# Attention probabilities left unscaled, their reciprocal sums folded into the transposes

## The chip, the cores and the metric

The kernel runs on one core of one Trainium2 chip. The metric is the device time of one execution in microseconds (us). Engines are named as the profile names them: PE is TensorE (PEld its weight loads), DVE is VectorE, ACT is ScalarE, POOL is GpSimd, SP is the engine that issues the DMAs.

## The reference, cut to what matters

One inference step of a two-layer backbone on 128 context tokens and 512 latent tokens, in float32. In each layer a mixer of three head groups (mLSTM, gated linear attention, latent attention) is followed by an output projection, a layer norm, a SwiGLU feed-forward part and a second layer norm. The change is inside the third head group:

```python
def block(args):
    qnb, qrb = args
    s = jnp.einsum('bhqd,bhkd->bhqk', qnb, k_nope) + jnp.einsum('bhqr,bkr->bhqk', qrb, k_rope)
    p = jax.nn.softmax(s.astype(jnp.float32) * A_SCALE, axis=-1)
    return jnp.einsum('bhqk,bhkv->bhqv', p.astype(v.dtype), v)
```

There are 8 heads. The 512 latent queries (four tiles of 128) read 640 keys: 128 cached ones and the 512 latent ones. The 128 context queries read the 128 context keys only.

## The kernel before, in words

A layer goes through the input projections, the mLSTM group, the gated linear group, the latent attention (four pairs of heads), the output projection (`accd` tiles), and the feed-forward part (`pg`, `pu`, `accd`). `mm` (L60) is every product, `act` (L46) every ScalarE operation, `tt` (L49) every elementwise operation of two tensors, `ts` (L53) one with a scalar for each partition. Three products of `F32R` pairs for each step (`mm3`) make up most of PE's work; the value products `O`, the scan products `hnum` and `go` and the broadcasts `Mb` are products of plain `F32` tiles.

For a head h and a query tile t of 1 to 4, `scores` does this: six `F32R` products make the scores in the PSUM tile `sp` (128 x 640, two buffers); DVE takes the negated row maximum `nm`; ACT writes the exponentials into `Pt` (128 x 640) and the row sums into `sums`; DVE makes the reciprocal `rc`; and `Pt` is multiplied by `rc` in place, on POOL for t of 1 to 3 and on DVE for t of 4. `ptile` then makes, for each of five key tiles kt, the transposed probabilities `PT` (128 keys x 512 queries): four PE transposes, one for each query tile, into a PSUM tile with two buffers, then one copy to SBUF, on ACT for even kt and on DVE for odd kt. `values` multiplies `PT` with the values `Vt` into `O`. `prompt_scores` does the same for the context queries with the tiles `Pp` and `PTp`; it scales `Pp` on POOL, and the change leaves it alone.

The loop at the end of `mixer` goes over four pairs of heads; what order the instructions get on each engine is set by the framework's scheduler, which moves them between pairs. Before the attention, a few tiles are prepared: `cko` (a copy of the context latents that goes out by DMA) and `nc_` (the cached latents and rotary keys, which come in by DMA). They lie in the pool `qa`, on the side of SBUF that also gets the attention's tiles. `g0` is the pool of the gated linear group, whose tag `kx` (two buffers, `gla_ends`) is used before.

Of the kernel before, what the change touches and what calls it, by code (L numbers as in the profile page):

```python
# [6 lines left out]
F32 = mybir.dt.float32  # L7
# [28 lines left out]
def build(nc, tc, I, O, dbg=None, layers=L, stop=None):  # L36
    V, S, P, T = nc.vector, nc.scalar, nc.gpsimd, nc.tensor

    def dma(out, in_):
        return nc.sync.dma_start(out=out, in_=in_)  # L40

    def pool(name, bufs=1, **kw):
        return tc.tile_pool(name=name, bufs=bufs, reuse_waits="tile", **kw)

    def act(out, in_, f, **kw):
        return S.activation(out=out, in_=in_, func=f, **kw)  # L46

    def tt(out, a, b, op, e=V):
        return e.tensor_tensor(out=out, in0=a, in1=b, op=op)  # L49

    def ts(out, a, s1, s2, o0, o1=None, e=V):
        if o1 is None:
            return e.tensor_scalar(out, a, s1, None, op0=o0)  # L53
        return e.tensor_scalar(out, a, s1, s2, op0=o0, op1=o1)
# [4 lines left out]
    def mm(out, lhsT, rhs, start=True, stop=True):  # L59
        return T.matmul(out, lhsT, rhs, start=start, stop=stop)  # L60

    def mm3(out, a, b, start, stop):
        mm(out, a[0], b[0], start, False)
        mm(out, a[0], b[1], False, False)
        mm(out, a[1], b[0], False, stop)
# [8 lines left out]
    ADD, SUB, MUL, MAX, MIN = ALU.add, ALU.subtract, ALU.mult, ALU.max, ALU.min  # L74
# [28 lines left out]
    def pa(name="pa"):  # L103
        return pt("a", name)

    def pb(name="pb"):
        return pt("b", name)

    def pq(name="pq"):
        return pt("q", name)  # L110
# [18 lines left out]
    ident = cst.tile([128, 128], F32, name="ident")  # L129
# [185 lines left out]
    def hsplit(h, l, src, e=V):  # L315
        act(h, src, AF.Copy)
        tt(l, src, h.bitcast(F32), SUB, e=e)
# [5 lines left out]
    def mixer(l, hT, adas, pm0, ws=None):  # L323
# [11 lines left out]
        g0 = g0s.enter_context(pool(f"glas{l}"))  # L335
# [57 lines left out]
        else:  # L393
            todo = [(g, f) for g in range(2) for f in first]
            for part in (todo[:5], todo[5:]):
                accs = [pt("aabbb"[i], "acc") for i in range(len(part))]
                for kk in range(4):
                    for acc, (g, ((src, M), (wh, wl), dst)) in zip(accs, part):
                        h, lo = hT[g]
# [74 lines left out]
        for i, (src, sc) in enumerate(((I_, -1.0), (e_, KSC), (eg, 1.0))):  # L474
            tr = pb("tokT")
# [21 lines left out]
        for t in range(NT):  # L497
            tr = pb("kT")
# [3 lines left out]
        def pos2tile(d, j):  # L502
            return 0 if j == 0 else (j if d == 0 else 5 - j)
# [5 lines left out]
        for j in range(0, 4):  # L509
            for d in range(2):  # L510
                t = pos2tile(d, j)
# [21 lines left out]
        for t in range(NT):  # L533
# [17 lines left out]
            for p in range(2):  # L551
                sq = pq("qk")
                for hh in range(2):
                    h = 2 * p + hh
# [164 lines left out]
        for j in range(0, 4):  # L719
            next(q2)  # L720
            for d in range(2):
                t = pos2tile(d, j)
# [133 lines left out]
        qp = lat2.enter_context(pool(f"qa{l}", side="right"))  # L856
# [4 lines left out]
        tr = pa("ckT")  # L861
        T.transpose(tr[:, 0:128], akv[:, 0:128], ident)
        T.transpose(tr[:, 128:160], misc[0:32, 0:128], ident[0:32, 0:32])
        cko = qp.tile([128, 160], F32, name="cko")
        V.tensor_copy(cko, tr[:, 0:160])
        dma(O["ckv"][l], cko[:, 0:128])
        dma(O["kr"][l], cko[:, 128:160])
        for i in range(2):
            hsplit(cq[0][:, i], cq[1][:, i], acq[i])
        nc_ = qp.tile([128, 128], F32, name="nc_")  # L870
        dma(nc_, I["ckvT"][l])
        for dst, src in ((slice(0, 128), akv[:, 0:128]), (slice(128, 256), nc_), (slice(256, 768), akv[:, 128:640])):
            hsplit(ckv[0][:, dst], ckv[1][:, dst], src)
# [22 lines left out]
        qp = lat2.enter_context(pool(f"qb{l}", side="right"))  # L896
# [58 lines left out]
        Qs, Ps, Pp = {}, {}, {}  # L955
# [37 lines left out]

        def scores(h):
            q, k = Qs[h], Kt[h % 3]
            for t in range(1, NT):
                sp = pq("sp")
                for cc in range(2):
                    tc_, kc = slice(t * 128, (t + 1) * 128), slice(128 + cc * 320, 448 + cc * 320)
                    mm3(sp[:, cc, 0:320], (q[0][:, tc_], q[1][:, tc_]), (k[0][:, kc], k[1][:, kc]), True, True)  # L1000
                nm = qp.tile([128, 1], F32, tag="nm", bufs=4, name="nm")
                V.tensor_reduce(nm, sp[:, :, 0:320], AX.XY, MAX, negate=True)
                Pt = (ap if h % 2 else qp).tile([128, 640], F32, tag="Pt", bufs=5, name="Pt")
                act(Pt.rearrange("p (a b) -> p a b", a=2), sp[:, :, 0:320], AF.Exp, bias=nm,
                    accum_out=sums[:, t, h:h + 1])
                rc = qp.tile([128, 1], F32, tag="rc", bufs=4, name="rc")
                V.reciprocal(rc, sums[:, t, h:h + 1])
                tt(Pt, Pt, rc.to_broadcast([128, 640]), MUL, e=P) if t % 4 else ts(Pt, Pt, rc, None, MUL)
                Ps[h, t] = Pt

        def prompt_scores(p):
            sp = pb("spp")
# [16 lines left out]
        def ptile(h, kt):  # L1029
            tr = pb("PT")  # L1030
            for t in range(1, NT):
                T.transpose(tr[:, (t - 1) * 128:t * 128], Ps[h, t][:, kt * 128:(kt + 1) * 128], ident)  # L1032
            PT = ap.tile([128, 512], F32, tag="PT", bufs=8, name="PT")
            if kt % 2:
                V.tensor_copy(PT, tr)
            else:
                act(PT, tr, AF.Copy)
            return PT

        def values(p, PA):  # L1040
# [24 lines left out]
            for kt in range(NT):  # L1065
                PB[kt] = ptile(2 * p + 1, kt)
                if kt == 0:
                    prompt_T()
                if kt not in (1, 4):
                    continue  # L1070

                ins = None
                ks = (1, 0) if kt == 1 else (4, 3, 2)
                for k in ks:
                    for hh in (1, 0):
                        h = 2 * p + hh
                        with tc.issue_after(ins.ins) if ins else nullcontext():
                            i_ = mm(O_[64 * hh:64 * hh + 64, :], Vt[:, 1 + k, h * 64:(h + 1) * 64], (PA[k], PB[k])[hh],
                                    k == 1, k == 2)
                        ins = ins or i_  # L1080
                if kt == 1:
                    with tc.issue_after(ins.ins):
                        prompt_O()
# [4 lines left out]
        proj(0, True)  # L1088
        run(chain(vals(), rope(1)))
        scores(0)  # L1090
        run(mix_T())
        persist.close()
        am = ExitStack()
        ap = am.enter_context(pool(f"am{l}"))
        for p in range(4):
            scores(2 * p + 1)
            prompt_scores(p)
            PA = [ptile(2 * p, kt) for kt in range(NT)]
            if p < 3:
                proj(p + 1)  # L1100
            values(p, PA)
            if p < 3:
                scores(2 * p + 2)
# [241 lines left out]
    for t in range(NT):  # L1345
        r = p0.tile([128, 1024], F32, tag="xrow", bufs=NT, name="xrow")
        dma(r, xin(t))
        for hf in range(2):
            tr = pb("hTt")
# [14 lines left out]
    for qt in range(NQ):  # L1364
# [19 lines left out]
        tr = ada_[:, 1, qt * KQ * 64:(qt + 1) * KQ * 64]  # L1384
# [19 lines left out]
    for l in range(layers):  # L1404
        mixT = mixer(l, hT, adas if l == 0 else iter(()), pm if l == 0 else None, ws if l == 0 else None)
        hT = tail_half(l, mixT, xin if l == 0 else (lambda t: xsp[t]), adan)
# [143 lines left out]
```

## Time and profile before

| | us |
|---|---|
| median of 3 runs | 1842.28 (1838.88 to 1842.68) |
| the profiled execution, its own time | 1843.47 |
| its span, first to last instruction | 1841.7 |
| PE busy | 1739.3 (94%) |
| DVE busy | 1039.5 (56%) |
| ACT busy | 701.9 (38%) |
| POOL busy | 331.3 (18%) |

The busy time of an engine is the union of its instructions' times. On PE the instructions overlap: the end of a matmul is modelled, and the next one starts before it. So the time between the starts of two matmuls, not the duration of one, tells how long PE was taken by it. A row of the timeline that merges n equal instructions gives the first start and the time to the last end; that time less one duration, over n - 1, is the distance between starts.

### The profile page before, as it was taken

Reading aid. Unit: us, or ns where it says so; the run is one execution under the profiler, and the core shown is the slowest. Engines: PE = TensorE matmul, PEld = TensorE weight load, DVE = VectorE, ACT = ScalarE, POOL = GpSimd, SP = SyncE. Lnnn points to the kernel's source line nnn. Section 1 sums busy time; section 2 is a strip of 40 time slices with the busy share of each in tenths; the row PEclk is TensorE's granted clock in tenths of the full one; section 3 lists DMA queues with packets and bytes.
Section 4 is the critical chain, followed back from the end, with each engine's and each line's share of the span. In section 5 each row is a group of like instructions: output and inputs, shape, how many; then the busy total and the mean of one; then the engine's idle time right before and its main releaser. Section 6 shows DMA issues by size and latency. Waiting matters only on the chain.

```text
span 1841.7 us, 28757 instructions
## 1 busy us (share of the span) xinstructions
PE 1739.3 (94%) x11360; PEld 1528.5 (83%) x11360; DVE 1039.5 (56%) x1888; ACT 701.9 (38%) x1490; POOL 331.3 (18%) x280
## 2 busy tenths in 40 slices
PE   8999988989999999999988999898999999999996
PEld 4877877768999899899878888676789989989995
DVE  3536377757588757564476366776465334333237
ACT  4345465743422122122243556576152212222221
POOL 0002352421430000000032126235026000000003
PEclk9989999999999999999998899999999999999998
DMA  9644431033256445343223223201412222213211
GB/s 323 214 132 144 147 89 41 17 122 109 97 157 204 141 138 162 119 127 97 79 80 123 26 62 96 68 17 38 172 69 92 71 79 81 69 59 95 76 58 57
DMA packets 83830, 190.96 MB, mean 104 GB/s; under 512 B 13864, under 2 KB 29512, under 8 KB 81648
## 3 DMA queue, kind: packets, MB, share of 16 engines
q1 hardware_dynamic: 83696, 189.14, 33.3%
q8 instruction: 89, 1.46, 0.3%
q14 instruction: 45, 0.37, 0.1%
HBM read 174.27 MB, written 5.70 MB: 98 GB/s over the span
## 4 chain that ended last, share of the span: by engine, by line
PE 79%; DVE 9%; DMA 5%; ACT 4%; issue 2%; POOL 2%; SPq 0%; DVEq 0%; ACTq 0%; POOLq 0%
PE accd L60 21%; PE pu L60 16%; PE pg L60 16%; PE acc L60 6%; PE accB L60 5%; PE sp L60 2%; PE O L60 2%; DMA araw<-w_ada 2%; PE ada L60 2%; POOL x L49 1%; PE PT L1032 1%; PE hnum L60 1%; PE ep L60 1%; ACT Pt L46 1%; PE go L60 1%
## 5 line engine op out<-in xcount | busy, mean ns | idle before, releaser
L46 ACT ACTIVATE wh<-raw 128x1024 fp32r<-128x1024 f32 (+2 forms) x193 | 197.3, 1027 | 545.2 <-PE accd L60 229.8
L49 DVE TENSOR_TENSOR wl<-raw,wh 128x1024 fp32r<-128x1024 f32 (+2 forms) x175 | 218.3, 1250 | 305.3 <-ACT wh L46 301.8
L60 PE MATMUL pg<-l,wh 128*128 128x256 f32 (+1 forms) x704 | 219.9, 312 | 8.6 <-DVE l L49 8.6
L60 PE MATMUL pu<-h,wl 128*128 128x256 f32 (+1 forms) x704 | 218.0, 310 | 1.4 <-POOL wl L49 1.4
L60 PE MATMUL pg<-h,wh 128*128 128x256 f32 (+1 forms) x704 | 219.2, 312 | 0.0
L60 PE MATMUL pg<-h,wl 128*128 128x384 f32 (+1 forms) x704 | 219.0, 312 | 0.0
L60 PE MATMUL pu<-l,wh 128*128 128x256 f32 (+1 forms) x704 | 218.3, 310 | 0.0
L60 PE MATMUL pu<-h,wh 128*128 128x256 f32 (+1 forms) x704 | 218.3, 310 | 0.0
L49 POOL TENSOR_TENSOR x<-x,lrow 128x512 f32<-128x512 f32 (+1 forms) x22 | 42.0, 1932 | 826.2 <-PE hTt L281 415.0
L60 PE MATMUL accd<-wl,gh 128*128 128x512 f32 x440 | 173.3, 394 | 0.0
L60 PE MATMUL accd<-wh,gh 128*128 128x512 f32 x440 | 171.7, 393 | 0.0
L60 PE MATMUL accd<-wh,gl 128*128 128x512 f32 x440 | 170.8, 390 | 0.0
L60 PEld LDWEIGHTS pg<-l,wh 128*128 128x128 f32 x704 | 134.4, 191 | 10.4 <-DVE l L49 9.0
L60 PEld LDWEIGHTS pu<-h,wl 128*128 128x128 f32 x704 | 134.2, 191 | 1.8 <-POOL wl L49 1.8
L60 PEld LDWEIGHTS pg<-h,wh 128*128 128x128 f32 x704 | 134.5, 191 | 1.4 <-issue 1.2
L60 PEld LDWEIGHTS pg<-h,wl 128*128 128x128 f32 x704 | 134.3, 191 | 1.1 <-issue 1.0
L60 PEld LDWEIGHTS pu<-l,wh 128*128 128x128 f32 x704 | 134.5, 191 | 0.0
L60 PEld LDWEIGHTS pu<-h,wh 128*128 128x128 f32 x704 | 134.2, 191 | 0.0
L57 DVE SCALAR_TENSOR_TENSOR aacc<-araw,scT,aacc 128x512 f32<-128x512 f32 x168 | 118.0, 746 | 14.9 <-DMA araw<-w_ada 14.8
L49 DVE TENSOR_TENSOR sg<-sg,pu 128x256 f32<-128x256 f32 (+1 forms) x88 | 42.7, 486 | 118.8 <-PE pu L60 118.7
L60 PE MATMUL accB<-wh,h 128*128 128x256 f32 x320 | 96.8, 302 | 2.8 <-DVE acq L57 2.2
L60 PEld LDWEIGHTS accd<-wh,gh 128*128 128x128 f32 x440 | 82.7, 188 | 19.2 <-issue 0.6
(359 smaller groups left out, 3710.3 us busy)
## 6 DMA issues: line engine op xcount, KB each, us to landing
araw<-w_ada SPq DMA_DIRECT2D x128, 256.0 KB
raw<-w_gate SPq DMA_DIRECT2D x44, 512.0 KB
raw<-w_up SPq DMA_DIRECT2D x44, 512.0 KB
raw<-w_down SPq DMA_DIRECT2D x40, 512.0 KB
araw<-w_ada SPq DMA_DIRECT2D x16, 1024.0 KB
raw<-w_inB SPq DMA_DIRECT2D x16, 512.0 KB
raw<-w_out SPq DMA_DIRECT2D x16, 512.0 KB
raw<-w_inA SPq DMA_DIRECT2D x12, 512.0 KB
```

Of the source, the lines that this page charges most:

```text
L46: return S.activation(out=out, in_=in_, func=f, **kw)
L49: return e.tensor_tensor(out=out, in0=a, in1=b, op=op)
L57: return e.scalar_tensor_tensor(out=out, in0=a, scalar=s, in1=b, op0=o0, op1=o1)
L60: return T.matmul(out, lhsT, rhs, start=start, stop=stop)
L1032: T.transpose(tr[:, (t - 1) * 128:t * 128], Ps[h, t][:, kt * 128:(kt + 1) * 128], ident)
```

## The change

`Pt` stays as the exponentials left it. For each head a tile `dg` (four 128 x 128 slices, two buffers) takes, for each query tile, the identity matrix times `rc`, always on POOL. The transpose of a 128 x 128 piece of `Pt` by the identity becomes a product of that piece with the slice of `dg`, as a plain `F32` matmul. To make room for `dg`, `cko` and `nc_` move into buffers of the tag `kx` in the pool `g0`.

```diff
-        cko = qp.tile([128, 160], F32, name="cko")
+        cko = g0.tile([128, 2, 128], F32, tag="kx", bufs=2, name="cko").rearrange("p a b -> p (a b)")[:, 0:160]
...
-        nc_ = qp.tile([128, 128], F32, name="nc_")
+        nc_ = g0.tile([128, 2, 128], F32, tag="kx", bufs=2, name="nc_")[:, 0]
...
         def scores(h):
             q, k = Qs[h], Kt[h % 3]
+            dg = qp.tile([128, 4, 128], F32, tag="dg", bufs=2, name="dg")
...
                 rc = qp.tile([128, 1], F32, tag="rc", bufs=4, name="rc")
                 V.reciprocal(rc, sums[:, t, h:h + 1])
-                tt(Pt, Pt, rc.to_broadcast([128, 640]), MUL, e=P) if t % 4 else ts(Pt, Pt, rc, None, MUL)
-                Ps[h, t] = Pt
+                tt(dg[:, t - 1], ident, rc.to_broadcast([128, 128]), MUL, e=P)
+                Ps[h, t] = Pt, dg[:, t - 1]
...
             for t in range(1, NT):
-                T.transpose(tr[:, (t - 1) * 128:t * 128], Ps[h, t][:, kt * 128:(kt + 1) * 128], ident)
+                mm(tr[:, (t - 1) * 128:t * 128], Ps[h, t][0][:, kt * 128:(kt + 1) * 128], Ps[h, t][1])
```

The scheduler gives a new order, in the attention and in the few operations just ahead of it. On PE, around the key projections `kacc` for the second pair of heads of layer 0 (`PTp` are the context queries' transposes, `sp` the next scores, `O` and `Op` the value products):

```order
-L1032 MATMUL PT<-ident,Pt 128x128 x8
+L60 MATMUL PT<-dg,Pt 128x128 x8
 L60 MATMUL kacc<-ckvh,wh 128x384
 L60 MATMUL kacc<-ckvl,wh 128x384
 L60 MATMUL kacc<-ckvh,wl 128x384
-L1032 MATMUL PT<-ident,Pt 128x128 x11
-L1055 MATMUL PTp<-ident,Pp 128x128 x2
-L1032 MATMUL PT<-ident,Pt 128x128
+L60 MATMUL PT<-dg,Pt 128x128 x4
```

The operations stand one for one, under another line and with `dg` in the place of `ident`; the long run of eleven transposes is cut into fours by the second key projection.

On POOL, in the attention of layer 0 from the third pair of heads on (`wl` are the first three weight pieces of the output projection, split on POOL):

```order
+L49 TENSOR_TENSOR dg<-ident,rc 128x128
+L49 TENSOR_TENSOR wl<-raw,wh 128x1024
+L49 TENSOR_TENSOR dg<-ident,rc 128x128 x2
 L49 TENSOR_TENSOR wl<-raw,wh 128x1024 x2
-L49 TENSOR_TENSOR Pt<-Pt,rc 128x640 x2
+L49 TENSOR_TENSOR dg<-ident,rc 128x128 x3
+L49 TENSOR_TENSOR Pp<-Pp,rc_4252 128x256
+L49 TENSOR_TENSOR dg<-ident,rc 128x128 x5
 L49 TENSOR_TENSOR wl<-raw,wh 128x1024 x5
```

Operations on 128 columns stand where those on 640 stood, one for every query tile, and the weight splits still stand between them.

On DVE, ahead of the attention of layer 0 (`graw` is a gate's raw value, `go` the last product of the gated linear group):

```order
 L49 TENSOR_TENSOR wl<-raw,wh 128x1024
 L656 COPY graw<-accB 128x256
+L865 COPY cko<-ckT 128x160
 L49 TENSOR_TENSOR wl<-raw,wh 128x1024
 L816 COPY qh_1312<-go 128x256
```

The copy into `cko` stood some twenty operations later before, behind the last `go` copy; it no longer waits for the memory that the gated linear group gives up.

## Rows read from the trace of the kernel before

**Rows 1.** The page: busy time, share of the span, instructions of each engine.

```profile
PE 1739.3 (94%) x11360; PEld 1528.5 (83%) x11360; DVE 1039.5 (56%) x1888; ACT 701.9 (38%) x1490; POOL 331.3 (18%) x280
```

**Rows 2.** Busy time and granted clock in the two attention stretches (start:end, length).

```profile
310.00:400.00 90.00, 80.51 (x516) 61.05 (x516) 65.26 (x140) 60.95 (x144) 38.13 (x30) 1.00 0.10 28
1202.00:1297.00 95.00, 85.14 (x530) 63.62 (x529) 64.84 (x139) 61.45 (x146) 38.21 (x30) 0.98 0.10 26
```

**Rows 3.** The chain that ended last, its shares by line from 300 to 402 us.

```profile
by line: PE sp L60 21.5%; PE O L60 18.2%; PE PT L1032 11.3%; ACT Pt L46 7.8%; DVE nm L1002 4.5%; PE qacc L60 4.5%; DVE PT L1035 3.3%; ACT PT L46 3.0%; PE racc L60 2.6%; ACT h L46 2.4%; issue 2.3%; PE spp L60 2.1%; DVE acq L49 1.6%; ACT K L4
```

**Rows 4.** Timeline of PE: start, time to the last end, operation, count.

```profile
333.20 1.04 PE L1032 MATMUL PT<-ident,Pt 128*128 128x128 f32 x8
...
336.60 2.80 PE L60 MATMUL O<-PT,Vt 128*64 128x512 f32 x12
...
382.76 2.80 PE L60 MATMUL O<-PT,Vt 128*64 128x512 f32 x12
```

**Rows 5.** Instructions of the tile PT: ns minimum/median/maximum, first and last start.

```profile
L1032 PE MATMUL PT<-ident,Pt x320: 270/273/476, 310.2 to 1293.1; 128*128 128x128 f32 x160
L60 PE MATMUL O<-PT,Vt x160: 592/593/645, 328.4 to 1296.2; 128*64 128x512 f32 x160
L46 ACT ACTIVATE PT<-PT x48: 577/597/599, 320.2 to 1293.4; 128x512 f32<-128x512 f32 x48
L1035 DVE COPY PT<-PT x32: 670/681/693, 322.7 to 1292.8; 128x512 f32<-128x512 f32 x32
```

**Rows 6.** Other plain F32 products, by tile, as in rows 5.

```profile
L60 PE MATMUL hnum<-v,Dt x160: 218/275/478, 129.7 to 1091.3; 128*128 128x65 f32 x160
L60 PE MATMUL hnum<-C,qi x32: 380/383/642, 141.6 to 1079.1; 128*128 128x260 f32 x32
...
L60 PE MATMUL go<-gv,At x80: 219/275/444, 243.6 to 1176.1; 128*128 128x64 f32 x80
...
L60 PE MATMUL Mb<-rowM,ident x160: 269/271/578, 111.8 to 1072.3; 32*128 32x128 f32 x160
```

**Rows 7.** Timeline of PE where such products stand in a row.

```profile
143.47 0.60 PE L60 MATMUL hnum<-C,qi 128*128 128x260 f32 x2
...
150.95 1.15 PE L60 MATMUL Mb<-rowM,ident 32*128 32x128 f32 x8
152.04 1.11 PE L60 MATMUL hnum<-v,Dt 128*128 128x65 f32 x8
...
243.60 1.00 PE L60 MATMUL go<-gv,At 128*128 128x64 f32 x8
```

**Rows 8.** The scaling of Pt and Pp, by tile.

```profile
L49 POOL TENSOR_TENSOR Pt<-Pt,rc x48: 1242/1253/1522, 308.3 to 1285.4; 128x640 f32<-128x640 f32 x48
L53 DVE TENSOR_SCALAR Pt<-Pt,rc x16: 533/546/1151, 317.9 to 1286.5; 128x640 f32<-128x640 f32 x16
...
L49 POOL TENSOR_TENSOR Pp<-Pp,rc x8: 612/613/751, 321.7 to 1280.1; 128x256 f32<-128x256 f32 x8
```

**Rows 9.** POOL by line and shape: busy us, mean ns, idle before.

```profile
L49 POOL TENSOR_TENSOR wl<-raw,wh 128x1024 fp32r<-128x1024 f32 x18 | 42.8, 2387 | 133.3 <-ACT wh L46 128.5 <-issue 4.7
L49 POOL TENSOR_TENSOR Xk<-EK,kg 128x128 f32<-128x128 f32 x70 | 33.7, 515 | 16.7 <-issue 10.2 <-ACT EK L46 6.5
```

**Rows 10.** PE's waits, 309 to 400 us: total, times, longest.

```profile
PE sp L60 <- ACT Pt L46: 2.7, 4, 1.3
...
PE PT L1032 <- DVE rc L1007: 0.4, 1, 0.4
...
PE kacc L60 <- DVE Qh L49: 0.2, 1, 0.2
```

**Rows 11.** The same from 1201 to 1297 us.

```profile
PE PT L1032 <- DVE PT L1035: 2.2, 3, 1.1
...
PE PT L1032 <- DVE PTp L1056: 0.3, 1, 0.3
```

**Rows 12.** Who waited for the tile cko.

```profile
PE racc L60: 1.2, 2
```

## Prediction

> **What bounds the kernel now.** I read the page first. PE is busy for 94% of the span, no other engine for more than 56% [rows 1]. The change acts in the attention alone, so the next view is the busy time in the two stretches where it runs, one in each layer: PE 80.5 of 90 us and 85.1 of 95 us, DVE 65.3 and 64.8, ACT 61.0 and 61.5, POOL 38.1 and 38.2 [rows 2]. The granted clock there is 1.00 and 0.98, so PE runs at the upper of its two levels, 2.4 GHz, almost throughout. A busy PE is not a full PE, so I then read the chain that ended last in the first stretch: the score products, the value products and the transposes `PT` hold 51% of it, while ACT's exponentials hold 7.8% and DVE's maxima 4.5% [rows 3]. The scaling of `Pt` is not among the lines named there. Last come PE's waits. In layer 0 the view has ten rows, 8.8 us together, the longest group for the exponentials that free `sp` [rows 10]; in layer 1 nine rows, 9.2 us [rows 11]. That is 18.0 us in all. Of the scaling of `Pt` they name only 0.4 us, a wait for `rc` [rows 10]. So in this part PE sets the pace, and DVE, ACT and POOL have room.
>
> One more row gives the beat: the last six value products of a pair of heads (twelve records) start at 336.60 us and, two pairs later, at 382.76 us [rows 4], so a pair of heads takes 23.1 us.
>
> **What goes.** 48 POOL operations of 1253 ns (60.1 us) and 16 on DVE of 546 ns (8.7 us) [rows 8]. POOL waits for work most of the time, so its 60 us are worth nothing by themselves; DVE has 25 us free in the 90 [rows 2].
>
> **What comes on POOL.** 64 products of the identity with `rc`, 128 x 128. The trace has none. `Pt` at 640 columns takes 1253 ns and `Pp` at 256 takes 613 [rows 8], a line through 400 ns at 128; `Xk`, two tensors of this very size, takes 515 ns [rows 9]. I take 0.45 us: 64 of them are 29 us, 31 less on POOL than now. The latency from `rc` to the first transpose falls from 1.25 to 0.45 us. But the query tile that DVE scaled now passes through POOL too, behind the weight splits `wl` of 2.39 us [rows 9]. There are three of them among the attention's POOL operations in each layer, so such a wait can come to 2.4 to 7.2 us a layer, if PE has nothing else to do then. PE has: the scores and projections of the next pair.
>
> **What comes on PE.** This decides. A `PT` transpose is one record in the trace: 8 heads by 5 key tiles by 4 query tiles by 2 layers are 320, and 320 records there are [rows 5]. A plain F32 product is two. `O` is issued 8 x 5 x 2 = 80 times and has 160 records [rows 5]; `hnum<-v,Dt` 4 heads x 2 directions x 5 tiles x 2 layers = 80, and 160 records; `Mb` likewise [rows 6]. So the 320 transposes become 640 records.
>
> What does one take? Eight transposes in a row take 1.04 us to the last end, one lasts 0.273, so the starts are 0.77 / 7 = 0.110 us apart [rows 4, 5]. For products with 128 moving columns and full weights the trace has no row, but neighbours on both sides: 65 columns, (1.11 - 0.275) / 7 = 0.119; 64 columns, (1.00 - 0.275) / 7 = 0.104; 128 columns on 32 rows, (1.15 - 0.271) / 7 = 0.126; and two records of 260 columns stand 0.60 - 0.380 = 0.22 us apart, or 0.108 for 128 columns [rows 6, 7]. I take 0.112, between them, with 0.104 and 0.126 as bounds. A product then takes 0.224 us where the transpose took 0.110: 0.114 more, 36.5 us for 320. The bounds give 31.4 and 45.4 us.
>
> The Trainium skill speaks against this change more strongly. Its page "TensorE: Matmul & The Clock Gate", in the section Terms, says that the transpose mode is four times faster for FP32. The record counts above say two, at nearly the same distance; by the page the cost would be that of the last rival below.
>
> **What of it is hidden.** In a pair of heads the 40 products take 9.0 us instead of 4.4, so 23.1 us become 27.7 if nothing gives way. DVE's and ACT's work for a pair stays as it is or falls, so they fall behind less: PE's waits are for copies of `PT`, for the exponentials and for `K`, `Qh` and `l` pieces, all on engines that are idle 25 to 30 of 90 us [rows 2, 10, 11]. The `PT` copies take 0.60 and 0.68 us [rows 5]; four transposes pass in 0.44 us, so PE can outrun two buffers now. Four products take 0.90 us, more than either copy, so this kind of wait should mostly go. Waits that come straight behind PE's own work (the last `PT` of a pair, then its copy, then `O`) stay. I count half of the 18.0 us as recovered: 9. The extremes are none and all.
>
> **The smaller parts.** DVE's 8.7 us and the shorter latency are already in that half; they help the same waits. The copy into `cko` moves ahead, out of the place where `racc` waited 1.2 us for it in two pieces [rows 12]: 1 us gained. `nc_` is loaded earlier and `kx` was last used by transposes long before: nothing, covered by the whole scan group between them. Outside the attention and the operations just ahead of it the order on every engine is unchanged: nothing.
>
> **The sum.** 1843.5 (the profiled execution; its span is 1.8 less, which lies around it) + 36.5 - 9 - 1 = 1870.0. The median of the runs shown is 1.2 us below that execution, so I forecast 1868.8, put as 1869 us, 1.4% slower.
>
> **Rivals.**
>
> *Nothing is hidden.* The waits are latencies that no longer products shorten, and the products take the upper bound: 45.4 - 1, about 1887 us. A POOL wait behind `wl` of 2.4 us in each layer would take it to 1891. For it: the waits behind the last `PT`. Against: DVE and ACT are idle for a quarter or more of the stretch.
>
> *All is hidden that can be.* The lower bound with all waits recovered: 31.4 - 18.0 - 1 = 12.4, about 1855 us. For it: the new order gives PE longer runs of work. Against: PE is never free of chains through one other engine.
>
> *Faster: the scaling, not PE, holds the beat.* If the chain through maxima, exponentials, `rc` and scaling set the pace of every query tile, then DVE's 8.7 us and POOL's 0.8 us for the last tile of each of 16 heads (12.8 us) would come back whole, while PE's extra is covered: 1842.3 - 21.5, about 1821 us. It decides if a product costs less than 21.5 / 320 = 0.067 us more than a transpose, or if PE has that much free. Against: the waits name 0.4 us for `rc` and nothing else of the scaling, and 18.0 us of free PE are less than 31.4.
>
> *No change.* A product of a diagonal runs as one record like the transpose (the change costs PE nothing): 1842 less a few us of latency, inside 0.2% or just faster. Against: every plain F32 product in the trace has two.
>
> *Four times a transpose.* A product takes 4 x 0.110 = 0.44 us: 0.33 x 320 = 105.6 us more, about 1938 us with half the waits recovered. This is what the Trainium skill's page gives (same title and section). Rows 5 and 6 bear against it.
>
> **How the numbers follow.** The forecast, around half of the waits recovered, 1858 to 1880 us: 0.74. Nothing hidden: 0.08. All hidden: 0.08. Faster: 0.04. No change: 0.03. Four times: 0.03. The range is 1854 to 1886 us, from all waits recovered at the lower bound to nearly none at the upper. A measurement of this kernel tells about 0.2% from no change, 3.7 us. Slower by more: 0.74 + 0.08 + 0.08 + 0.03 = 0.93. Within it: 0.03. Faster: 0.04.
>
> **What the profile after would show.** `PT` with 640 records about 0.11 us apart; PE records 11680. DVE busy down by 8.7 us, POOL by some 31. The beat of a pair of heads from 23.1 to 26 or 27 us, the two stretches 10 to 15 us longer each, and everything else in place. PE's waits for `PT` copies should shrink, the ones for the exponentials less. I am wrong if `PT` keeps 320 records, if the distance of its records is far from 0.11 us, or if a new row of PE waiting for `dg` or for POOL stands at the top of the waits.

## The result, and the profile after

The changed kernel takes 1858.12 us (median of 4 runs, 1852.9 to 1863.88) where the kernel before takes 1840.58 (4 runs, 1838.2 to 1842.68): 1.009 times as long, 95% interval 1.0072 to 1.0109. It is slower, by 17.5 us where 26.5 were forecast. Five more runs of it in a later experiment (e9 below) gave 1863.67 us, 1.0121 times the kernel before, interval 1.0104 to 1.0139.

The page of the changed kernel, against [rows 1]:

```profile
span 1853.1 us, 29406 instructions
## 1 busy us (share of the span) xinstructions
PE 1758.8 (95%) x11680; PEld 1557.5 (84%) x11680; DVE 1033.7 (56%) x1872; ACT 703.9 (38%) x1490; POOL 295.6 (16%) x296
```

PE has 320 records more and 19.5 us more of busy time; DVE lost 16 instructions and 5.8 us, POOL 35.7 us. The tiles `PT` and `dg`, against [rows 5, 8] (ns minimum/median/maximum, first and last start):

```profile
L60 PEld LDWEIGHTS PT<-dg,Pt x640: 186/192/193, 305.5 to 1304.9; 128*128 128x128 f32 x160
L60 PE MATMUL PT<-dg,Pt x640: 270/275/377, 305.6 to 1305.0; 128*128 128x128 f32 x160
...
L46 ACT ACTIVATE PT<-PT x48: 580/597/602, 312.8 to 1305.4; 128x512 f32<-128x512 f32 x48
L1037 DVE COPY PT<-PT x32: 673/692/693, 315.3 to 1304.4; 128x512 f32<-128x512 f32 x32
```

```profile
L49 POOL TENSOR_TENSOR dg<-ident,rc x64: 398/401/406, 303.7 to 1298.2; 128x128 f32<-128x128 f32 x64
```

A diagonal takes 0.401 us on POOL. The timeline of PE, around the place of [rows 4]:

```profile
330.44 1.95 PE L60 MATMUL PT<-dg,Pt 128*128 128x128 f32 x16
334.76 2.80 PE L60 MATMUL O<-PT,Vt 128*64 128x512 f32 x12
...
343.60 1.95 PE L60 MATMUL PT<-dg,Pt 128*128 128x128 f32 x16
```

```profile
384.55 2.79 PE L60 MATMUL O<-PT,Vt 128*64 128x512 f32 x12
```

Sixteen records take 1.95 us to the last end, so they stand (1.95 - 0.275) / 15 = 0.112 us apart. The last value products of a pair of heads start at 334.76 us and, two pairs later, at 384.55: a pair takes 24.9 us, where it took 23.1.

The two attention stretches, from the last `go` product to the end of the value products, of the changed kernel and then of the kernel before (start:end, length, busy time of PE, PEld, DVE, ACT and POOL, granted clock, DMA):

```profile
279.90:407.90 128.00, 118.13 (x801) 98.20 (x800) 81.66 (x169) 76.40 (x179) 27.15 (x44) 1.00 0.11 30
1180.90:1308.90 128.00, 118.20 (x801) 98.47 (x801) 81.50 (x169) 77.31 (x181) 27.09 (x44) 1.00 0.12 30
```

```profile
285.70:402.30 116.60, 103.06 (x642) 78.93 (x640) 84.33 (x178) 75.27 (x180) 45.18 (x36) 1.00 0.13 34
1176.20:1296.90 120.70, 105.82 (x641) 81.19 (x641) 84.63 (x178) 76.32 (x181) 44.33 (x36) 0.97 0.13 33
```

The stretches are 11.4 and 7.3 us longer, 18.7 together; the second figure is the smaller because the clock fell in layer 1 before (0.97) and not after. The span grew by 11.4 us only: outside the stretches this execution is 7.3 us shorter, 5.9 of them ahead of the first `go` product (at 237.7 instead of 243.6 us), where the change does nothing. PE is free for 9.9 and 9.8 us, where it was free for 13.5 and 14.9. The chain through the attention of layer 0 tells the same, against [rows 3] (300 to 402 us, shares by line):

```profile
by line: PE PT L60 30.4%; PE sp L60 27.4%; PE O L60 15.4%; PE qacc L60 4.3%; ACT Pt L46 2.5%; PE kacc L60 2.2%; PE spp L60 1.8%; ACT PT L46 1.8%; DVE nm L1003 1.6%; ACT K L46 1.3%; PE mxT L943 1.3%; DVE PT L1037 1.3%; issue 1.2%; DVE Qh L49
```

`PT` went from 11.3% to 30.4%, the exponentials from 7.8% to 2.5%, the maxima from 4.5% to 1.6%: the detours through ACT and DVE are what the products now cover. PE's waits in that attention, whole, against [rows 10]:

```profile
PE O L60 <- DVE PT L1037: 0.8, 1, 0.8
PE sp L60 <- ACT Pt L46: 0.7, 2, 0.4
PE O L60 <- ACT PT L46: 0.7, 1, 0.7
PE PT L60 <- DVE PTp L1058: 0.5, 1, 0.5
PE kacc L60 <- DVE Qh L49: 0.5, 1, 0.5
PE sp L60 <- ACT K L46: 0.5, 1, 0.5
PE PT L60 <- DVE PT L1037: 0.4, 1, 0.4
```

And in layer 1, against [rows 11]: first one more row of the kernel before, then the list of the changed kernel, whole:

```profile
PE sp L60 <- ACT Pt L46: 1.8, 3, 1.3
```

```profile
PE sp L60 <- ACT Pt L46: 1.9, 3, 0.9
PE O L60 <- DVE PT L1037: 0.8, 1, 0.8
PE O L60 <- ACT PT L46: 0.7, 1, 0.7
PE PT L60 <- DVE PTp L1058: 0.5, 1, 0.5
PE PT L60 <- POOL dg L49: 0.3, 1, 0.3
PE sp L60 <- ACT K L46: 0.2, 1, 0.2
```

In layer 0 4.1 us are left of 8.8, in layer 1 4.4 of 9.2. The exponentials that free `sp` hold 0.7 instead of 2.7 in layer 0, but in layer 1 as much as before, 1.9 and 1.8. What is left of the waits for `PT` copies is mainly, in each layer, the 0.8 and 0.7 us that `O` waits for the last `PT` tiles of a pair, straight behind PE's own work.

### The profile page after: what moved, and what is told of

Read it like the earlier page. It is cut to its first block, busy times and chain, and to the rows that moved or that the text cites. A ratio compares the mean times of both kernels' runs of the same rounds, so it can differ in the third digit from the quotient of the medians.

```text
span 1853.1 us, 29406 instructions
## 1 busy us (share of the span) xinstructions
PE 1758.8 (95%) x11680; PEld 1557.5 (84%) x11680; DVE 1033.7 (56%) x1872; ACT 703.9 (38%) x1490; POOL 295.6 (16%) x296
## 4 chain that ended last, share of the span: by engine, by line
PE 81%; DVE 8%; DMA 4%; ACT 3%; POOL 2%; issue 2%; SPq 0%; DVEq 0%; ACTq 0%; POOLq 0%
PE accd L60 21%; PE pu L60 16%; PE pg L60 16%; PE acc L60 5%; PE accB L60 5%; PE PT L60 4%; PE sp L60 3%; PE O L60 2%; PE ada L60 2%; POOL x L49 1%; DMA araw<-w_ada 1%; PE hnum L60 1%; PE ep L60 1%; PE go L60 1%; PE lv L60 1%
```

## Two measures that the comparisons use

Single executions of one kernel lie up to 14 us apart here (1852.9 to 1867.35 over the nine of the changed kernel). Most of that is the granted clock: the profiled execution of before has a mean clock of 0.972, that of the changed kernel 0.980, and much of the difference lies in stretches far from the change, as those 5.9 us. So two more measures are used. The *time at the upper clock* is an execution's time multiplied by its mean granted clock, and the median of that; the rest is what the clock cost. The clock is given to three places, so one execution is uncertain by 0.9 us; where the clock falls while PE waits anyway, the product takes off too much. The nine executions of the changed kernel lie within 1811.1 to 1817.8 us by it. The *attention at the upper clock* is the time from the first `PT` record to the last `O` record of a layer, multiplied by the clock of that window, and added up over the two layers of the profiled execution. These are the windows, two of the kernel before and two of the changed kernel:

```profile
310.25:401.76 91.51, 82.02 (x524) 61.38 (x522) 65.01 (x139) 60.95 (x144) 38.13 (x30) 1.00 0.10 27
1202.65:1296.24 93.59, 83.73 (x523) 62.74 (x522) 64.19 (x138) 60.68 (x144) 38.21 (x30) 0.98 0.10 27
```

```profile
305.63:407.34 101.71, 97.62 (x683) 80.77 (x682) 61.11 (x130) 62.14 (x144) 21.65 (x38) 1.00 0.09 25
1206.71:1308.20 101.49, 97.03 (x683) 80.97 (x682) 61.26 (x130) 62.07 (x144) 21.83 (x38) 1.00 0.09 25
```

| kernel | time, us (runs) | ratio to before, 95% | at the upper clock | cost of the clock | attention at the upper clock |
|---|---|---|---|---|---|
| before (beside e1 to e4) | 1841.57 (23) | | 1789.9 | 53.4 | 183.2 |
| changed | 1858.12 (4) | 1.0072 to 1.0109 | 1814.7 | 43.7 | 203.2 |
| changed, again (e9) | 1863.67 (5) | 1.0104 to 1.0139 | 1813.4 | 50.3 | 203.3 |
| e1 products by the identity | 1860.43 (6) | 1.0092 to 1.0135 | 1813.8 | 47.4 | 205.1 |
| e2 no scaling | 1836.34 (12) | 0.9957 to 1.0014 | 1789.3 | 46.8 | 179.9 |
| e3 the move alone | 1843.79 (12) | 1.0005 to 1.0042 | 1794.1 | 51.7 | 182.1 |
| e4 products twice | 1923.94 (4) | 1.0423 to 1.0488 | 1873.9 | 48.2 | 267.3 |
| e5 one pass | 1852.06 (12) | 1.0017 to 1.0075 | 1788.5 | 63.9 | 177.2 |
| e6 diagonals on DVE | 1861.42 (6) | 1.0062 to 1.0132 | 1813.8 | 47.5 | 204.2 |
| e7 transposes twice | 1862.15 (6) | 1.0071 to 1.0142 | 1811.9 | 50.3 | 203.3 |
| e10 one pass, twice | 1867.83 (4) | 1.0125 to 1.0164 | 1813.1 | 56.0 | 203.0 |
| e11 one pass, DVE | 1847.34 (12) | 1.0016 to 1.0044 | 1793.1 | 54.5 | 183.0 |

The kernel before was timed again beside e5 to e7 (1842.99 us, 1789.8 at the upper clock) and beside e9 to e11 (1841.06 and 1790.2).

## The experiments

**e1_product_ident: the products alone.** The kernel before, with the scaling of `Pt` as it was.

```diff
-                T.transpose(tr[:, (t - 1) * 128:t * 128], Ps[h, t][:, kt * 128:(kt + 1) * 128], ident)
+                mm(tr[:, (t - 1) * 128:t * 128], Ps[h, t][:, kt * 128:(kt + 1) * 128], ident)
```

> The kernel before with one edit: the transposes become plain F32 products with the identity; Pt is scaled as before, 48 times on POOL and 16 times on DVE. My theory after the result: the products cost PE 36.5 us in full, PE's waits of 18 us take up about half of it, and the lighter scaling does next to nothing. Then this kernel is as slow as the changed one or up to 3 us slower, 1858 to 1862 us. The rival, that the lighter scaling (8.7 us of DVE, 0.8 us of latency a tile) gave the missing half back: 1866 to 1872 us.

Measured: 1860.43 us, and 1813.8 at the upper clock, as the changed kernel (1813.4 and 1814.7). The products alone make a loss as large as the whole change's. What the change takes off POOL and DVE gives 2 us in the attention (205.1 to 203.2) and nothing that the whole time shows; the move, which this kernel doesn't have, costs about as much (e3).

**e2_no_scaling: the scaling left out.** The kernel before with its transposes; reciprocal and scaling of `Pt` are left out, so the output is that of unscaled probabilities.

```diff
-                rc = qp.tile([128, 1], F32, tag="rc", bufs=4, name="rc")
-                V.reciprocal(rc, sums[:, t, h:h + 1])
-                tt(Pt, Pt, rc.to_broadcast([128, 640]), MUL, e=P) if t % 4 else ts(Pt, Pt, rc, None, MUL)
```

> The kernel before with the reciprocal and the scaling of Pt left out; transposes by the identity stay, so the attention of the latent queries stays undivided by its sums. It is the scaling's whole price with PE's work untouched. My theory (PE sets the pace, scaling is hidden): at most 4 us faster than before, 1836 to 1841 us. The rival (the lighter scaling is worth 8 us or more): 1825 to 1832 us.

Measured: 1836.34 us, ratio 0.9957 to 1.0014; the attention is 3.3 us shorter (183.2 to 179.9), the whole at the upper clock 0.6 us. That bounds what any cheaper scaling can give here: 5 us of 1842 by the medians, 8 by the end of the interval, and the change replaced it by work on the engine that sets the pace.

**e3_move_only: `cko` and `nc_` in `kx`.** The kernel before, with the two lines of the move alone.

```diff
-        cko = qp.tile([128, 160], F32, name="cko")
+        cko = g0.tile([128, 2, 128], F32, tag="kx", bufs=2, name="cko").rearrange("p a b -> p (a b)")[:, 0:160]
...
-        nc_ = qp.tile([128, 128], F32, name="nc_")
+        nc_ = g0.tile([128, 2, 128], F32, tag="kx", bufs=2, name="nc_")[:, 0]
```

> The kernel before with cko and nc_ in buffers of kx, and nothing else. I put 1 us on this move: 1839 to 1840.5 us, not told from no change. A rival, that the move is what gave back several us ahead of the attention: 1833 to 1837 us.

Measured: 1843.79 us, 1.0005 to 1.0042 times before; the 1 us gained of the sum isn't there. PE's waits ahead of the attention of layer 0 show why. First the kernel before (285.7 to 309 us), then this one (280.8 to 306 us):

```profile
PE vacc L60 <- ACT Vt L46: 1.7, 2, 1.3
PE vacc L60 <- ACT acq L46: 1.2, 1, 1.2
PE racc L60 <- DVE cko L865: 0.6, 1, 0.6
PE racc L60 <- DVE cql L49: 0.3, 1, 0.3
```

```profile
PE vacc L60 <- ACT Vt L46: 2.8, 1, 2.8
PE vacc L60 <- ACT acq L46: 1.6, 1, 1.6
PE racc L60 <- DVE cql L49: 0.9, 1, 0.9
```

The wait for `cko` is gone, and the next ones are longer: 3.8 us have become 5.3. (The clock in this place was 0.88 here; in the changed kernel, at 1.00, these waits hold 5.7 us.) Why ACT's tiles come later was not traced. Where the clock was 1.00, the first `PT` record of layer 0 comes 24.3 to 24.6 us after the last `go` in three kernels without the move (before, e2, e7), and 25.7 to 25.8 us after it in three with it (the change, e4, e6). In layer 1 it is 25.1 us in the one without (e7), and 25.8 to 26.6 in four with it (the change, e3, e6, e9). So the move costs some 1 us a layer in that place, 2 us in all. The whole time of this kernel shows 2.2 us as run (1843.79 against 1841.57) and 4.2 at the upper clock (1794.1 against 1789.9). The reverse, the change without the move, was not tried, since the move makes the room for `dg`.

**e4_products_twice: twice the suspected cost.** The changed kernel with each product issued twice.

```diff
                 mm(tr[:, (t - 1) * 128:t * 128], Ps[h, t][0][:, kt * 128:(kt + 1) * 128], Ps[h, t][1])
+                mm(tr[:, (t - 1) * 128:t * 128], Ps[h, t][0][:, kt * 128:(kt + 1) * 128], Ps[h, t][1])
```

> The changed kernel with every product into PT issued twice, the second writing the same values again. If PE's waits took up the missing half and are used up, the 320 further products cost their full 0.224 us: 71.7 us more, 1922 to 1932 us. If about half of any PE work added here is hidden, 36 us more: about 1894 us. If a product costs PE less than its spacing says, less still.

Measured: 1923.94 us. The attention grew by 64.1 us (203.2 to 267.3) for 320 x 0.224 = 71.7 us of products: nine tenths show. Of the first 36.5 us only 20.0 showed (183.2 to 203.2). So what products can hide in is limited here, and the change had used up most of it.

**e5_one_pass: half the records.** The changed kernel with `Pt` and `dg` as `F32R`, so that a product is one record ("one-pass"); probabilities and reciprocals are rounded to that type by it.

```diff
-            dg = qp.tile([128, 4, 128], F32, tag="dg", bufs=2, name="dg")
+            dg = qp.tile([128, 4, 128], F32R, tag="dg", bufs=2, name="dg")
...
-                Pt = (ap if h % 2 else qp).tile([128, 640], F32, tag="Pt", bufs=5, name="Pt")
+                Pt = (ap if h % 2 else qp).tile([128, 640], F32R, tag="Pt", bufs=5, name="Pt")
```

> The changed kernel with Pt and dg held as F32R, so that a product of a diagonal is one pass instead of a plain F32 product's two; the probabilities and reciprocal sums are rounded to F32R by it, which changes the computation. Theory (the second record of each product is the whole price, and the scaling is worth a few us at most): PT has 320 records, the distance of two is about the 0.112 us of one record now, the stretches fall from 254.9 us together to 229 to 238 us, and the time to 1835 to 1842 us, at or up to 5 us below the kernel before. Rival (it is the new order, the passage through POOL or the heavier weight loads, and not the number of records): the time stays at 1852 to 1860 us though the records halve.

Measured: 1852.06 us, a miss of 10 us by the theory, and inside the range of its rival. But the reasons of the rival don't show at the upper clock: the records halved, and the time went back whole, to 1788.5 us. (The attention's 177.2 us, less even than without any scaling, can be too low, since the clock fell in it and PE also waited.) The time was lost again to the clock: 63.9 us instead of some 53, with the clock falling inside the attention, where it held in the changed kernel. Tile `PT`, then two windows of e5:

```profile
L60 PE MATMUL PT<-dg,Pt x320: 220/275/477, 307.3 to 1296.4; 128*128 128x128 f32 x160
```

```profile
340.00:369.00 29.00, 26.15 (x172) 21.20 (x170) 20.81 (x46) 22.66 (x52) 9.63 (x14) 0.99 0.15 38
...
393.50:406.50 13.00, 12.31 (x37) 5.32 (x38) 0.98 (x2) 1.51 (x4) 0.00 (x0) 0.51 0.00 0
```

The records are one for each product. From 393.5 to 406.5 us PE was busy for 12.31 of 13 us, with 37 records, at a granted clock of 0.51, near the lower level of 1.2 GHz.

**e6_diag_on_dve: POOL out of the path.** The changed kernel with the diagonals built on DVE.

```diff
-                tt(dg[:, t - 1], ident, rc.to_broadcast([128, 128]), MUL, e=P)
+                ts(dg[:, t - 1], ident, rc, None, MUL)
```

> The changed kernel with the diagonals built on DVE, straight behind the reciprocal, instead of on POOL. Theory (POOL's part is off the path: PE waited 5.6 us for dg in the whole execution, mostly where other work was lacking too): within 3 us of the changed kernel, 1855 to 1861 us. Rival (the passage through POOL, behind the weight splits, is part of the loss): 5 us or more faster, 1853 us or less. Third case (DVE's time is what sets the beat with its copies and maxima): 4 us or more slower, 1862 us or more.

Measured: 1861.42 us, 0.4 us outside the theory's range and short of the third case; at the upper clock 1813.8, as the changed kernel. Where the diagonals are built makes no difference here.

**e7_transposes_twice: the same PE time without any product.** The kernel before, each transpose issued twice.

```diff
                 T.transpose(tr[:, (t - 1) * 128:t * 128], Ps[h, t][:, kt * 128:(kt + 1) * 128], ident)
+                T.transpose(tr[:, (t - 1) * 128:t * 128], Ps[h, t][:, kt * 128:(kt + 1) * 128], ident)
```

> The kernel before with each transpose into PT issued twice, the second over the first; scaling and everything else as before. It adds 320 records of a transpose at 0.110 us, 35.2 us of PE, as the change did with its 36.5 us, but no plain F32 product, no diagonal and no other weights. Theory (the loss is PE time alone, of which half vanishes in waits that were there): 1856 to 1862 us, stretches 252 to 258 us together, as with products. Rival (a plain product costs more than its distance shows, by its weight load of 0.19 us or by changes of kind between products): 1852 us or less.

Measured: 1862.15 us, 1811.9 at the upper clock, attention 203.3 us: the theory to within 0.2 us of its range, and the rival's 1852 is far off. Records of PE that compute nothing new cost the same as the change: 20.1 us show of 35.2. Neither the kind of record nor its weight load (192 ns for a product, 140 for a transpose) adds to the distance.

**e9_after_again: the changed kernel unaltered, for its clock.**

> The changed kernel once more, unaltered, for more samples of its time and its granted clock (four so far: mean clock 0.973, 0.973, 0.980 and 0.980). A run's time multiplied by its mean granted clock is its time had the clock stayed at the upper level; the rest is what the clock cost. So far the kernel before has 1789.8 us and some 52 us of clock, the changed kernel 1814.7 and 43.7. Theory (the change costs about 25 us at the upper clock, as the sum forecast, and denser PE work loses less to the clock): again 1813 to 1816 us at the upper clock, 42 to 46 us of clock, 1856 to 1860 us. Rival (the four samples had luck with the clock, and nothing is given back): the same at the upper clock, but 50 to 54 us of clock, 1864 to 1868 us. Other rival (half the waits do not come back, more do): 1810 us or less at the upper clock.

Measured: 1863.67 us, 1813.4 at the upper clock, 50.3 us to the clock. The time at the upper clock repeats; the 43.7 us of the first four runs don't. The theory is right in the first and wrong in the second; the first rival (luck with the clock) is nearer, at the edge of its ranges. The profiled executions, the first set's at 1853.1 us and this one at 1865.6, are of one program, so each PE record of one has its partner in the other. One stretch of 74 records around the `hnum` products of layer 1, ahead of the attention, first there and then here:

```profile
1073.54:1084.73 11.19, 10.31 (x74) 8.65 (x75) 10.90 (x36) 8.61 (x30) 3.05 (x2) 1.00 0.11 40
```

```profile
1080.05:1097.32 17.27, 17.27 (x74) 15.16 (x75) 11.98 (x43) 9.98 (x31) 3.03 (x2) 0.51 0.07 28
```

Near the lower level it took 6.1 us longer. Another 5.9 us had come about within the first 200 us, and only 1.0 between the two around the attention of layer 0. So the two executions of one program differ mostly where the change does nothing. Over the nine runs the clock cost 50.3 us (median), against 51.6 to 53.4 for the kernel before beside the experiments: what the denser work gives back through the clock is 1 to 3 us, if anything.

**e10_one_pass_twice: 640 one-pass records.** The kernel of e5 with each product issued twice (the added line of e4). Probabilities and reciprocals are rounded as in e5.

> The kernel with Pt and dg as F32R, whose products are one record, with each product issued twice, the second over the first: 640 one-pass records, as many as the changed kernel has (probabilities and reciprocal sums are rounded to F32R). Theory (the number of records is the price, whatever their kind): 1810 to 1816 us at the upper clock, 22 to 27 more than with 320 (1788.5), 1856 to 1866 us as run, and less lost to the clock than the 64 us with 320. Rival (one-pass records let the clock fall by themselves): still 60 us or more of clock, 1872 us or more. Other rival (F32R products take less than 0.112 us): 1803 us or less at the upper clock.

Measured: 1867.83 us, 2 us above the theory's range, with 1813.1 us at the upper clock, inside it, and attention 203.0. The number of records is the price, whatever their kind. The clock cost 56.0 us, less than the 63.9 of e5, as the theory had it, and more than the 43.7 and 50.3 of the changed kernel.

**e11_one_pass_dve: e5 with the diagonals on DVE.** The edit of e6 on the kernel of e5, rounded as there.

> The kernel with Pt and dg as F32R (one-pass products) with the diagonals built on DVE, behind the reciprocal, not on POOL. With POOL it lost 64 us to the clock where the kernel before loses some 52, with dips of the clock inside the attention, and PE waited 8.3 us for dg. Theory (the waits behind POOL are among the gaps ahead of which the clock falls): lost to the clock 56 us or less, 1840 to 1847 us. Rival (the passage through POOL has no part in it): 60 to 67 us lost, 1849 to 1855 us. In both 1787 to 1791 us at the upper clock.

Measured: 1847.34 us, 0.3 us outside the theory's range, and 54.5 us to the clock, inside it; at the upper clock 1793.1, above the range of both. It lost 9.4 us less to the clock than e5, of which 1.8 went the same way in the kernel before beside it, but is 4.6 us longer than e5 at the upper clock. Against the kernel before, the two can't be told apart: 1.0016 to 1.0044 here, 1.0017 to 1.0075 for e5. And the clock fell in the attention without POOL in the path, here and in e3, which has no diagonals at all. The attention of layer 0 of e11, then of e3:

```profile
306.17:402.47 96.30, 87.03 (x524) 65.95 (x523) 66.93 (x161) 61.28 (x144) 9.53 (x7) 0.95 0.09 26
```

```profile
308.42:402.46 94.04, 85.02 (x523) 63.26 (x522) 65.11 (x139) 60.95 (x144) 38.13 (x30) 0.96 0.10 26
```

So that the passage through POOL makes the clock fall is not shown. The kernel is still slower than the kernel before. No version that was run is faster than the kernel before beyond its uncertainty.

## Why the prediction was right in direction and too high in size

*What bounds the kernel: right.* PE sets the pace of the attention: records that do nothing new (e7) cost as much as the change, removing all scaling (e2) gives next to nothing.

*The products: right in each number.* 640 records, 11680 in all, 0.112 us apart; 36.5 us of PE time added. The rival in which a product costs four times a transpose fell: 0.224 against 0.110 us is twice. That rival came from the Trainium skill, page "TensorE: Matmul & The Clock Gate", section Terms; this trace does not agree with its factor of four for FP32. The rival of one record fell with the count; e5 shows that it would have been free at the upper clock.

*POOL: right.* 0.401 us for a diagonal, where 0.45 was taken between 0.400 and 0.515; 35.7 us less instead of 31. Off the path (e6).

*DVE: nearly.* 8.7 us were forecast; 5.8 went, and where the other 2.9 us went was not traced.

*What is hidden: the term that was mis-sized.* "I count half of the 18.0 us as recovered: 9." The list of PE's waits did what was said of it: 8.5 of its 18.0 us are left, so 9.5 went. But the list doesn't measure what added work can hide in. In the attention 20.0 us show of 36.5, so 16.5 were hidden, 7.5 more than the sum took; some 2 of them are the lighter scaling (the products without it, e1, hide 14.6). PE's free time in the windows of the second measure fell from 19.4 to 8.6 us, by 10.8; the rest lies inside time that counted as busy. The starts of the records in the two traces show it. From each `PT` record to the start of PE's next record are 59.9 us in all for the 320 of the kernel before, and 79.0 for the 640 of the changed kernel. Less 0.110 and 0.112 us for each, PE stood behind them for 24.7 and 7.3 us: 17.4 less, the whole cover and a little of the clock that fell in layer 1 before. Of the 24.7 and 7.3 us, 17.4 and 5.9 are shown as free; the rest, 7.3 and 1.4, lies within the shown durations. A record is shown for 0.275 us and the next can start 0.112 us after it, so a short stall behind it is shown 0.16 us shorter, or not at all. The Trainium skill has this in "Perfetto Trace Analysis", section Per-engine timelines: the end of a TensorE instruction is estimated from its size and the SBUF delay, not observed. These sums agree with it.

*The move: wrong.* "1 us gained" for the earlier copy into `cko` was a loss, of some 2 us in the windows ahead of the attention and 2 to 4 in the whole time. The wait for `cko` went, as forecast, but PE then stood longer before the values' products, for ACT's `Vt` and `acq` and DVE's `cql` (e3). The step had counted a wait as gained without asking what was late next.

*The sum at the upper clock.* 36.5 - 16.5 and 2 to 4 for the move make 22 to 24; measured on the whole run are 23.6 (1813.5 over the nine runs, less 1789.9). The forecast of 26.5 was 3 us too high there. It came that near by luck: the cover was taken 7.5 us too small, and the move 3 to 5 us too favourably, which partly cancels.

*The clock: not in the sum.* The sum took the executions as equal in clock. The four runs that the result rests on lost 43.7 us to it, 8 to 10 less than the kernel before; the five of e9 lost 50.3. So of the 10.9 us between forecast and result, about 3 are this sum, 1.7 are the kernel before (1842.28 us ahead of the result, 1840.58 with it), and the rest, some 6, fits the clock in those four runs, which did not repeat. Against the 1863.67 us of e9 the forecast of 1869 was 5 us too high.

*The rivals.* "All is hidden" (1855 us) was nearest in the cover (16.5 of 18.0 us), but had the products at 31.4 us where they take 36.5; at the upper clock its 12.4 us are 11 too few, and the clock of the first four runs brought the measured time near it. "Faster" had no place: 2 us in the attention are all that the lighter scaling gave (e1). "Nothing is hidden" fell with e4 and e7. Of the signs named, the records and their distance came as said. The stretches are 11.4 and 7.3 us longer where 10 to 15 stood, the second short because the clock fell there before; the beat is 24.9 us where "26 or 27" stood, since more was hidden. There is no row of PE's matmuls waiting for POOL above 0.3 us in the attention.

## What to carry to other kernels

To fold an elementwise scaling into PE's transposes doubles their PE time when the data are plain F32, so it pays only where PE is not what sets the pace and the engine relieved is; here the relieved engines were busy for less than three quarters of the stretch. When work is added to the bounding engine, the list of its waits doesn't tell how much of it will be hidden: here the list gave back 9.5 of 18.0 us, and 16.5 were hidden. The starts of its records tell more: behind the `PT` records PE stood for 24.7 us before and 7.3 with the change, and of the next 72 us of products nine tenths showed (e4). Where a change is worth 1%, compare times at the same granted clock: two sets of four and five runs of one kernel lay 5.6 us apart as run and 1.3 us at the upper clock.

## What the runs showed of the hardware that was not expected

The clock can take back what PE saves. With one-pass products (e5) the attention had less PE work than the changed kernel's, and the clock fell in it: to 0.9 in layer 0 and 0.96 in layer 1 from the first `PT` to the last `O`, where the changed kernel had 1.00. PE was busy for nine tenths of the time ahead of such a fall (26.15 of 29 us). But the kernel before held 1.00 at the same share in layer 0 (80.51 of 90 us, [rows 2]). The clock fell with the diagonals on DVE too (e11), and in e3, where the same products ran as in the kernel before. What sets the fall is open.

A product's weight load of 192 ns, 52 longer than a transpose's, doesn't show in the distance between records: 0.112 against 0.110 us.
